# A block sum moved from GpSimd to an adding DMA, two splits moved ahead, and 64 bytes in front of a pair of tiles

## The chip, the cores and the metric

The kernel runs on one core of a Trainium2 chip. The time is that of one execution on the device, in microseconds; the median of three runs is given. The engines are TensorE (PE; PEld is its weight load), VectorE (DVE), ScalarE (ACT), GpSimd (POOL) and SyncE (SP). PE, DVE, ACT and POOL compute; SP issues transfers, and so does POOL, which here issues those that add to what is at their destination.

## What is computed

One layer of a decoder over 512 tokens and 16 learned tokens ahead of them, model width 1024, batch 1. Two branches read the same normalised input: retention (4 heads, keys of 256, values of 512) and gated linear attention (4 heads, keys of 128, values of 256). Their outputs are merged with sigmoid gates.

```python
u = rms_norm(h, norm_gain)
proj = u @ w_in
...
o_ret = retention_chunked(rq, rk, rv)
o_ret = head_group_norm(o_ret, ret_norm_gain.reshape(RET_HEADS, RET_V_DIM)).reshape(bsz, length, RET_WIDTH)
o_ret = o_ret * jax.nn.silu(rg)
...
o_gla = gla_chunked(gq, gk, gv, log_a)
o_gla = head_rms_norm(o_gla, gla_norm_gain.reshape(GLA_HEADS, GLA_V_DIM)).reshape(bsz, length, GLA_WIDTH)
o_gla = o_gla * jax.nn.silu(gg)

merged = jax.nn.sigmoid(m_ret) * (o_ret @ w_branch_ret) + jax.nn.sigmoid(m_gla) * (o_gla @ w_branch_gla)
return h + merged @ w_out
```

A final RMS norm follows. "The linear branch" below is `o_gla @ w_branch_gla`; "the heads' branch" is `o_ret @ w_branch_ret`.

## The kernel before

**Products in two parts.** Each float32 operand is split into a high part (a cast on ACT, L154) and a low part (the rest, a subtraction on DVE, also L154). A product is three matmuls: high by high, high by low, low by high. `split` makes both parts; `prepare` splits a weight block of 128x1024 and remembers the two instructions in `low`. The split weights rotate through three buffers for the high and three for the low parts.

**Seven products for eight.** `quad` multiplies two-by-two blocks by Strassen's scheme in Winograd's form: seven block products of 24 matmuls each, with sums of blocks on both sides. The weights' sums are made in place: w11 + x3, and w21 + w11 (L365), where x3 and x1 are themselves sums, made by a load from HBM by SP and a second load by POOL that adds (L280, L282). The other side's blocks and sums are the forms A11, A12, A22, S1, S2, S3, S4, here called `ga..` and `gs..`. The linear branch runs `quad` with `early=True` for two blocks of columns, j = 0 and j = 1, in the order of products 1, 7, 6, 2, 5, 4, 3. Three PSUM tiles, a, b and c (`bg_a`, `bg_b`, `bg_c`), collect them: product 6 adds to what product 1 left in b, after ACT has copied that out (L334), product 5 adds to b after the copy of product 6, product 4 adds to c after the copy of product 7. The copies go to two rotating buffers (`bg_x` in the trace, as the tiles x3 and x1 are). `put` adds a copy and a PSUM tile (L1160 to L1164) and sends the result to HBM.

**The forms of the linear branch.** `gla_sums` makes them while the branch already runs. `a00`, `a01`, `a10`, `a11` are the four blocks of the gated, transposed output of gated linear attention. The steps of `gla_sums` are woven with the products, one step after each product. `S2` is built from `a00`; after that `a01` becomes `a01 + a00` on POOL (L1115), and S4 is minus that sum: its high part on ACT (L1125), its low part on DVE (L1126). The forms S1 and A22 are placed behind the last weight split by `after`, which orders two instructions of one engine.

**The order of the work.** Instructions stand in each engine's queue in an order which the framework's planner works out from the program's order and its own cost estimates, unless `after` says otherwise. In the trace each engine runs its queue in that order, and an instruction that waits holds up those behind it.

**The heads' branch.** The turned (transposed) output of head h is kept in two tiles, `oh` and `ol`, of 8192 bytes a partition. Heads 0 to 2 share one pair in the pool `rp`, allocated at the first use in `ret_attention(0)`, the last tags of that pool; head 3's pair lies in the pool `cp`. `mm3` (L189, L192, L193) multiplies with them: the weights are stationary and `oh` or `ol` moves, 512 columns at a time, 8 products of 12 matmuls for each head.

## Time and profile before

| | |
|---|---|
| median of three runs | 761.6 us (761.6 to 762.16) |
| the profiled execution | 761.8 us, of which the span from the first to the last instruction is 760.0 us |
| PE busy | 749.8 us, 99% |
| DVE busy | 611.4 us, 80% |
| ACT busy | 450.8 us, 59% |
| POOL busy | 141.9 us, 19% |
| mean granted clock of PE | 0.997 |

In a timeline row stand the start and the length in us, the engine, the line, the operation, and what it writes and reads; in brackets the idle time before it and what ended that. A windows row gives, for a stretch of the span, the length, the busy time of each engine with the number of instructions that start there, the clock granted to PE, the busy share of the transfer engines and GB/s. In a row of waits stand the sum, the number and the longest. In a chain row stand start, length and what ran. In a row of transfers the last number is the time from issue to landing. A transfer's row on POOL shows the time in which POOL describes it, not the transfer itself. The ends of matmuls are modelled, so paces are read from starts.

### The profile page before, as it was taken

Reading aid. Unit: us, or ns where it says so; the run is one execution under the profiler, and the core shown is the slowest. Engines: PE = TensorE matmul, PEld = TensorE weight load, DVE = VectorE, ACT = ScalarE, POOL = GpSimd, SP = SyncE. Lnnn points to the kernel's source line nnn. Section 1 sums busy time; section 2 is a strip of 40 time slices with the busy share of each in tenths; the row PEclk is TensorE's granted clock in tenths of the full one; section 3 lists DMA queues with packets and bytes.
Section 4 is the critical chain, followed back from the end, with each engine's and each line's share of the span. In section 5 each row is a group of like instructions: output and inputs, shape, how many; then the busy total and the mean of one; then the engine's idle time right before and its main releaser. Section 6 shows DMA issues by size and latency. Waiting matters only on the chain.

```text
span 760.0 us, 14059 instructions
## 1 busy us (share of the span) xinstructions
PE 749.8 (99%) x5595; PEld 701.8 (92%) x5595; DVE 611.4 (80%) x873; ACT 450.8 (59%) x764; POOL 141.9 (19%) x172
## 2 busy tenths in 40 slices
PE   9999999999989999999999999999999999999996
PEld 6799899999989999999989999989999999988996
DVE  6799878689897789789957688966787989775994
ACT  7897584666974566546546555646464756532562
POOL 2211200112231122110530100440011210111142
PEclk9999999999999999999999999999999999999999
DMA  9864321822568972733783562794476356687503
GB/s 301 287 138 100 95 85 43 184 82 65 145 157 232 303 170 88 173 111 130 200 245 119 120 158 86 203 238 119 131 165 144 109 141 193 229 191 201 131 29 112
DMA packets 99994, 116.89 MB, mean 154 GB/s; under 512 B 5716, under 2 KB 90836, under 8 KB 99672
## 3 DMA queue, kind: packets, MB, share of 16 engines
q1 hardware_dynamic: 79896, 88.19, 36.7%
q0 software_dynamic: 19744, 27.27, 19.7%
q8 instruction: 44, 0.72, 0.4%
q10 hardware_dynamic: 288, 0.53, 0.2%
q14 instruction: 22, 0.18, 0.1%
HBM read 104.44 MB, written 11.53 MB: 153 GB/s over the span
## 4 chain that ended last, share of the span: by engine, by line
PE 91%; DVE 6%; issue 2%; ACT 1%; POOL 0%; POOLq 0%; DVEq 0%
PE rqk_b L318 6%; PE rv_b L318 6%; PE rg_b L318 6%; PE rqk_c L318 5%; PE br_p L189 4%; PE br_p L193 4%; PE br_p L192 4%; PE gg_b L318 3%; PE mr_b L318 3%; PE mg_b L318 3%; PE gv_p L640 3%; PE rv_c L318 3%; PE bg_b L318 3%; PE rg_c L318 3%; PE gg_c L318 2%
## 5 line engine op out<-in xcount | busy, mean ns | idle before, releaser
L189 PE MATMUL br_p<-oh,br_h 128*128 128x512 f32 x128 | 50.4, 394 | 0.0
L192 PE MATMUL br_p<-ol,br_h 128*128 128x512 f32 x128 | 50.4, 393 | 0.0
L193 PE MATMUL br_p<-oh,br_l 128*128 128x512 f32 x128 | 50.4, 393 | 0.0
L154 ACT CAST rv_h<-rv_w 128x1024 fp32r<-128x1024 f32 x24 | 25.3, 1052 | 27.1 <-DVE rv_w L371 9.6
L154 DVE TENSOR_TENSOR rv_l<-rv_w,rv_h 128x1024 fp32r<-128x1024 f32 x24 | 29.3, 1222 | 9.2 <-ACT rv_h L154 9.2
L154 DVE TENSOR_TENSOR rg_l<-rg_w,rg_h 128x1024 fp32r<-128x1024 f32 x20 | 24.4, 1222 | 8.7 <-ACT rg_h L154 8.7
L282 POOL DMA_DIRECT2D rqk_x<-in_w_in_dram x8 | 10.4, 1302 | 108.0 <-DVE rv_l L154 80.6
L154 ACT CAST rg_h<-rg_w 128x1024 fp32r<-128x1024 f32 x20 | 21.0, 1051 | 15.8 <-PE br_p L192 6.2
L193 PEld LDWEIGHTS br_p<-oh,br_l 128*128 128x128 f32 x128 | 24.0, 188 | 5.7
L189 PEld LDWEIGHTS br_p<-oh,br_h 128*128 128x128 f32 x128 | 24.0, 188 | 5.0
L192 PEld LDWEIGHTS br_p<-ol,br_h 128*128 128x128 f32 x128 | 24.0, 188 | 5.0
L154 ACT CAST br_h<-br_w 128x1024 fp32r<-128x1024 f32 x16 | 16.8, 1049 | 19.2 <-PE br_p L192 9.9
L154 ACT CAST rqk_h<-rqk_w 128x1024 fp32r<-128x1024 f32 x20 | 21.0, 1052 | 11.6 <-PE rqk_c L318 2.9
L1349 ACT ACTIVATE on<-av,nm,g_r 128x512 f32<-128x512 f32 x16 | 12.5, 780 | 25.4 <-DVE nm L1347 25.4
L318 PE MATMUL rv_b<-rv_l,fh 128*128 128x256 f32 x96 | 27.1, 282 | 0.2 <-DVE rv_l L154 0.2
L318 PE MATMUL rqk_b<-fh,rqk_h 128*128 128x256 f32 (+1 forms) x96 | 27.2, 283 | 0.0
L318 PE MATMUL rqk_b<-fh,rqk_l 128*128 128x256 f32 (+1 forms) x96 | 27.1, 283 | 0.0
L318 PE MATMUL rqk_b<-fl,rqk_h 128*128 128x256 f32 (+1 forms) x96 | 27.1, 282 | 0.0
L318 PE MATMUL rg_b<-rg_h,fl 128*128 128x256 f32 x96 | 27.0, 281 | 0.0
L154 DVE TENSOR_TENSOR rqk_l<-rqk_w,rqk_h 128x1024 fp32r<-128x1024 f32 x20 | 24.4, 1220 | 3.2 <-ACT rqk_h L154 3.2
L318 PE MATMUL rv_b<-rv_h,fl 128*128 128x256 f32 x96 | 27.0, 281 | 0.0
L318 PE MATMUL rg_b<-rg_h,fh 128*128 128x256 f32 x96 | 26.9, 281 | 0.0
(720 smaller groups left out, 3266.6 us busy)
## 6 DMA issues: line engine op xcount, KB each, us to landing
rv_w<-in_w_in_dram SPq DMA_DIRECT2D x16, 512.0 KB, 4.1
br_w<-in_w_branch_ret_dram SPq DMA_DIRECT2D x16, 512.0 KB, 3.4
rqk_w<-in_w_in_dram SPq DMA_DIRECT2D x12, 512.0 KB, 4.8
rg_w<-in_w_in_dram SPq DMA_DIRECT2D x12, 512.0 KB, 4.9
rqk_x<-in_w_in_dram SPq DMA_DIRECT2D x8, 512.0 KB, 3.9
rqk_x<-in_w_in_dram POOLq DMA_DIRECT2D x8, 512.0 KB, 8.2
rg_x<-in_w_in_dram SPq DMA_DIRECT2D x8, 512.0 KB, 3.7
rg_x<-in_w_in_dram POOLq DMA_DIRECT2D x8, 512.0 KB, 7.7
```

The source lines that it names most:

```text
L154: return nc.scalar.copy(hi, src), nc.vector.tensor_sub(lo, src, hi.bitcast(F32))
L189: m = nc.tensor.matmul(o, lh, rh, start=first, stop=False)
L192: nc.tensor.matmul(o, lh, rl, start=False, stop=False)
L193: m = nc.tensor.matmul(o, ll, rh, start=False, stop=last)
L282: x = nc.gpsimd.dma_start(t, block(0, 1), accum_op=ALU.add)
L318: m = nc.tensor.matmul(ps[t][:, :n] if wide else ps[t], l, r, start=first and j == 0, stop=kk == 3 and j == 2, skip_group_check=not fresh ...
L640: m = nc.tensor.matmul(pss[t], (al if j == 1 else ah)[t // 2, kh][:, k, c], (lo if j == 2 else hi)[:, kk, :], start=q == kk == j == 0, sto ...
L1349: nc.scalar.activation(on, ps, AF.Identity, scale=r, bias=nm)
```

## The change

The sum of two blocks is made by a transfer within SBUF that adds, issued by POOL: `a00 += a01` in place of `a01 += a00` on POOL's ALU. S4 is taken from `a00`, and its two instructions are placed behind the last weight split of their engines. In `quad` with `early=True`, the weights of product 5 are split right after those of product 2, ahead of w21 + w11, and the weights of product 3 right after those of product 4. At the first head, a tile of 64 bytes a partition is allocated ahead of `oh` and `ol` and set to zero by POOL.

```diff
@@ quad, early @@
             product(2, A12, w21, a, True)
-            nc.vector.tensor_add(w21, w21, w11)
+            ready = prepare(5, x1)
             put(0, 0, a, x)
             x7 = copy(c, 3)
             yield
+            nc.vector.tensor_add(w21, w21, w11)
...
-        product(5, S1, x1, b, False)
+        product(5, S1, x1, b, False, ready)
         put(1, 1, b, x7)
         run_late()
         yield
         product(4, A22, w21, c, False)
+        ready = prepare(3, w22) if early else None
         put(0, 1, c, y)
         yield
-        product(3, S4, w22, b, False)
+        product(3, S4, w22, b, False, ready)
@@ gla_sums @@
-        nc.gpsimd.tensor_add(a01, a01, a00)
+        nc.gpsimd.dma_start(a00, a01, accum_op=ALU.add)
...
         hi, lo = gforms[S4]
-        nc.scalar.mul(hi, a01, -1.0)
-        nc.vector.scalar_tensor_tensor(lo, a01, -1.0, hi.bitcast(F32), op0=ALU.mult, op1=ALU.subtract)
+        after(nc.scalar.mul(hi, a00, -1.0), low[0])
+        after(nc.vector.scalar_tensor_tensor(lo, a00, -1.0, hi.bitcast(F32), op0=ALU.mult, op1=ALU.subtract), low[1])
@@ ret_attention @@
+        if h == 0:
+            nc.gpsimd.memset(rp.tile([P, 16], F32, name="gap"), 0.0)
         oh, ol = [(rp if h < 3 else cp).tile([P, 4, T], F32R, tag=f"o{n}" if h < 3 else f"x{n}0", name=f"o{n}{h}")
                   for n in "hl"]
```

In the other branch of `quad` (without `early`) `ready` is set to `None` behind product 6, so nothing changes there.

## The prediction

> **What bounds the kernel now.** I read the page's busy shares and slices first, then the waits of PE, then the windows around the longest of them, then each engine's timeline there.

> ```profile
> PE 749.8 (99%) x5595; PEld 701.8 (92%) x5595; DVE 611.4 (80%) x873; ACT 450.8 (59%) x764; POOL 141.9 (19%) x172
> ...
> PE 91%; DVE 6%; issue 2%; ACT 1%; POOL 0%; POOLq 0%; DVEq 0%
> ...
> PE bg_b L318 <- DVE bg_l L154: 1.3, 1, 1.3
> ...
> PE bg_b L318 <- ACT bg_x L334: 0.8, 1, 0.8
> ```

> PE is busy for 99% of the span and holds 91% of the chain that ended last. A change can only gain by taking away one of PE's few waits or by making matmuls follow each other faster. Two of the three waits of 0.8 us or more stand next to each other, in the linear branch (tile `bg_b`); the third is at the start. The windows, cut where the granted clock changes, show that they cost more than their length:

> ```profile
> core 0: us, PE busy (x) PEld busy (x) DVE busy (x) ACT busy (x) POOL busy (x), PEclk, DMA share, GB/s
> 223.07:226.48 3.41, 1.43 (x10) 1.23 (x11) 3.41 (x5) 2.72 (x5) 0.00 (x0) 1.00 0.26 75
> 226.48:229.89 3.41, 3.41 (x19) 3.41 (x18) 3.09 (x4) 1.19 (x3) 0.00 (x0) 0.50 0.83 242
> 93.30:96.70 3.40, 2.93 (x21) 2.50 (x20) 3.27 (x10) 1.97 (x6) 0.99 (x2) 1.00 0.01 2
> ```

> PE was idle for 1.98 of the first 3.41 us, and through the next 3.41 us its clock was granted at 0.50 (19 matmuls started). An idle share of 0.47 us in 3.40 elsewhere left the clock at 1.00. Why PE waited is on the other engines:

> ```profile
> 218.67 1.22 DVE L154 TENSOR_TENSOR bg_l<-bg_w,bg_h 128x1024 fp32r<-128x1024 f32 x1
> 219.80 3.43 DVE L154 TENSOR_TENSOR gs<-og,gs 128x1024 fp32r<-128x1024 f32 x1
> 223.15 1.21 DVE L365 TENSOR_TENSOR bg_w<-bg_w,bg_w 128x1024 f32<-128x1024 f32 x1
> 224.29 1.21 DVE L154 TENSOR_TENSOR bg_l<-bg_x,bg_h 128x1024 fp32r<-128x1024 f32 x1
> ...
> 219.30 1.05 ACT L154 CAST bg_h<-bg_x 128x1024 fp32r<-128x1024 f32 x1
> 220.24 0.62 ACT L154 CAST ga22h<-og1gk 128x512 fp32r<-128x512 f32 x1
> 222.18 1.06 ACT L1125 ACTIVATE gs<-og1gq 128x1024 fp32r<-128x1024 f32 x1 [1.32 <-POOL og1gq L1115]
> 223.15 0.57 ACT L334 COPY bg_x<-bg_b 128x512 f32<-128x512 f32 x1
> ...
> 217.38 1.33 POOL L282 DMA_DIRECT2D bg_x<-in_w_branch_gla_dram  x1 [1.72 <-DVE gs L154]
> 218.84 3.30 POOL L1115 TENSOR_TENSOR og1gq<-og1gq,og 128x1024 f32<-128x1024 f32 x1
> ```

> The block sum on POOL (L1115) runs from 218.84 to 222.14. The DVE step that starts within it takes 3.43 us where the same form takes 1.22, and ends 1.1 us after POOL does: it stood still while POOL read SBUF. It pushes L365 and the low half of product 5's weights to 224.29, which is PE's wait of 1.3. ACT stands in front of L1125 for the same sum, and the copy of product 6's result, behind it in ACT's queue, is PE's wait of 0.8.

> **The change part by part.** *Block sum off POOL, product 5's weights split ahead.* The price of the jam is read from the same two products (2 and 5) of the next block of columns, which has no forms to make:

> ```profile
> 220.11 0.39 PE L318 MATMUL bg_a<-ga,bg_h 128*128 128x256 f32 x2
> ...
> 229.65 0.40 PE L318 MATMUL bg_c<-ga22h,bg_h 128*128 128x256 f32 x1
> ...
> 243.86 0.39 PE L318 MATMUL bg_a<-ga,bg_h 128*128 128x256 f32 x2
> ...
> 249.30 0.28 PE L318 MATMUL bg_c<-ga22h,bg_h 128*128 128x256 f32 x1
> ...
> 244.02 2.72 PE bg_a L318 x24
> ...
> 249.46 2.83 PE bg_c L318 x24
> ```

> 9.54 us against 5.44: 4.10 us too long, both waits and the half clock together (the last two rows, of the chain, give the length of one product of 24 matmuls). In the new order DVE runs, in steps of 1.13 (218.67 to 219.80): product 5's low half from 219.80, S1's low half from 220.95, done at 222.1. On ACT the casts of S1 and of x1 change places (x1's comes one step before 219.30), then come `ga22h` and, at about 220.9, the copy of product 6's result, with L1125 no longer ahead of it. PE wants product 5 at 222.83 (220.11 plus 2.72), so all 4.10 us go, if nothing else is late.

> *What is late next: product 4.* DVE has lost its slack. The steps that now come behind S1 and must be done before product 4:

> ```profile
> 225.42 0.68 DVE L154 TENSOR_TENSOR ga22l<-og1gk,ga22h 128x512 fp32r<-128x512 f32 x1
> 226.03 1.21 DVE L154 TENSOR_TENSOR bg_l<-bg_w,bg_h 128x1024 fp32r<-128x1024 f32 x1
> 227.16 0.68 DVE L1164 TENSOR_TENSOR gb<-bg_a,bg_x 128x512 f32<-128x512 f32 x1
> ...
> 227.87 0.59 ACT L334 COPY bg_x<-bg_c 128x512 f32<-128x512 f32 x1 [0.95 <-DVE gb L1164]
> ```

> L365 from 222.1, `ga22l` twice (0.60 each) to 224.45, L1164 to 225.1, product 4's low half to 226.25. The copy of product 7's result waits for L1164 (it needs the buffer that L1164 reads) and stands behind the cast of product 3's weights, which the change moves ahead (ACT to 225.4): done at 226.0. Product 5 ends at 225.55, so product 4 starts 0.5 us late, and its third matmul needs the low half at 226.25. If L1164 comes behind the low half, the copy ends at 226.8 and 1.25 us are lost; if it comes before `ga22l`, nothing. I take 0.6, between 0 and 1.3.

> *The sum as a DMA.* It needs S2's low half (the DVE step that released the row at 217.38) and stands in POOL's queue behind the accumulate at 217.38, so it is issued at 218.8, where the add starts now. No row shows an SBUF-to-SBUF add. The nearest are the accumulating loads of the same size, from issue to landing (issued at 206.7, 217.4 and 231.6):

> ```profile
> bg_x<-in_w_branch_gla_dram POOLq DMA_DIRECT2D x1, 512.0 KB, 5.8
> ...
> bg_x<-in_w_branch_gla_dram POOLq DMA_DIRECT2D x1, 512.0 KB, 6.5
> ...
> bg_x<-in_w_branch_gla_dram POOLq DMA_DIRECT2D x1, 512.0 KB, 10.4
> ```

> The middle one is just ahead of it in the same queue, with DMA share 0.26 after it; the slow one ran with the engines full. I take 7.5: landed at 226.3. S4's cast then runs behind the copy of product 7's result, from 226.3, and S4's low half on DVE behind product 3's low half (to 227.4) and L1162 (0.60, to 228.0): done at 229.2. Product 4 ends at 229.0 (225.55 + 0.6 + 2.83), so product 3 loses 0.2. A landing up to 226.95 costs no more; at 10.4 us (229.2) S4 is complete at 231.5, and 2.5 are lost instead of 0.2. No less than nothing is possible here.

> *Product 3's weights split ahead; L365 behind the split.* Both only change the order above: no instruction is added. In the next block of columns the split of x1 is bound by its landing:

> ```profile
> 242.12 1.05 ACT L154 CAST bg_h<-bg_x 128x1024 fp32r<-128x1024 f32 x1 [2.17 <-DMA bg_x<-in_w_branch_gla_dram]
> ...
> 225.53 0.37 SPq L280 DMA_DIRECT2D bg_x<-in_w_branch_gla_dram  x1
> ```

> It is ready at 244.45 and product 5 of that block starts at 246.58 (2.72 behind 243.86): 2.1 us of slack, where PE comes 3.3 earlier. But the load of x1 at 225.53 waits for L365 and the low half of product 5, which come 1.1 and 4.5 us sooner: some 1.5 us sooner on SP. I take 0, and 1.2 as the upper end (landing as now).

> *The 64-byte tile.* It is first used just ahead of `oh` and `ol` of heads 0 to 2, so it moves these two and nothing else that PE reads. Head 3's pair lies in another pool. Starts of PE's matmuls in the chain, head 2 and then head 3:

> ```profile
> 669.25 0.23 PE br_p L189
> ...
> 676.95 0.23 PE br_p L189
> 679.71 0.23 PE br_p L189
> ...
> 687.87 0.23 PE br_p L189
> ...
> 388.45 0.23 PE br_p L189
> ...
> 393.35 0.23 PE br_p L189
> ```

> Head 2: 11 groups of three matmuls in 7.70 us, 233 ns each. Head 3, same shape and same weights' buffers: 12 groups in 8.16 us, 227 ns. Head 0 (last two rows, 7 groups in 4.90): 233. So the pace hangs on where the moving operand lies. From the tiles' sizes `oh` and `ol` start at a multiple of 128 bytes, head 3's pair and the weights 64 bytes past one; 64 bytes bring heads 0 to 2 to head 3's place. 3 heads, 8 products of 12: 288 matmuls by 6.67 ns are 1.92 us, and PE is without a gap there. Bounds: 0, if the place is not the cause, and 1.92. [...]

> The tile's memset goes to POOL's queue:

> ```profile
> 249.88 0.87 POOL L1201 MEMSET km<- 128x256 f32 x1
> ```

> It has a sixteenth of that row's elements, so 0.87 is its upper end; POOL is idle 81% of the time. Cost 0; if it stood ahead of a head's power on POOL, 0.9 once.

> *Sum.* Gains 4.10 + 1.92, losses 0.6 + 0.2: 5.2 us. The profiled execution took 761.8 (span 760.0 and 1.8 around it), 0.2 above the median. 761.6 - 5.2 = **756.4**.

> **The rivals.** *The 64 bytes do nothing*: 758.3 (756.4 + 1.92). For it: head 3 also differs in its place in the program. Against: head 2 and head 3 stand within 20 us of each other at the two paces.

> *A new wait takes part of the place*: the sum lands late or L1164 and the copy come late, 2 to 2.3 us more (the 10.4 us row), and up to 4 with the half clock again (1.7 us: 3.41 at 0.50): 758.4 to 760.4. Whether it comes lies between the rows, 0.47 us idle without it and 1.98 with it. [...]

> *Slower: ACT queues S4's cast ahead of product 7's copy.* Then product 4 waits for the sum: it starts 1.74 us (1.06, 0.59 and a start) after the landing, at half clock after so long a wait (1.7). Against 229.65 before and with 1.92 gained, the point is a landing at 228.1, 9.3 us after issue; at 10.4 us the time is 762.7, and over 0.2% slower from 10.8 us. Against: the copy comes earlier in the program and its input (L1164) is ready first.

> *No change within 0.2%*: the PE lead made here is lost again to loads in the next blocks, whose transfers share engines that were 0.83 busy at 226.48: some 761. Against: the chain's rows at 244.02 and 249.46 stand 5.44 apart, twice 2.72, although x1 came off its load only at 242.12.

> **How the numbers follow.** Main case 0.60, with its own range 755.1 to 758.0 (losses from 0 to 2.4, product 6's small wait of 0.3 perhaps gone). The 64 bytes do nothing 0.10. New wait 0.19. Lead lost 0.06. Slower 0.05. About 0.2% (1.5 us) is what a measurement of this kernel can tell from no change. Of the new wait 0.03 lies above 760.1. Faster: 0.60 + 0.10 + 0.16 = 0.86; same 0.06 + 0.03 = 0.09; slower 0.05. The range 755.0 to 759.5 holds the main case, the first rival and most of the second.

> **What would show it.** Right: no PE wait over 0.3 us on product 5, no POOL add, every S1 low half at 1.2, L334 at 221, PEclk 1.00 through 226 to 230; heads 0 to 2 at 227 ns. Wrong: a PE wait on `bg_c` for L334 or on product 3 for S4, an ACT wait for the sum, a half-clock window about 226, heads 0 to 2 still at 233.

## The result, and the profile after

| | kernel before | kernel after |
|---|---|---|
| median | 761.74 us (761.6 to 762.16, 6 runs) | 758.16 us (757.25 to 759.11 but for one run, 6 runs) |
| ratio of times | | 0.9952, interval 0.9941 to 0.9963 |
| profiled execution | 761.8 us, span 760.0 | 759.11 us, span 757.3 |

One run of the kernel after took 4205 us, why is not known; it is left out of the ratio. In a second comparison the same kernel took 757.84 us (757.05 to 757.96, 5 runs), 0.9948 (0.9936 to 0.9961) of the kernel before. The change gains 3.6 to 3.8 us. The forecast was 756.4.

The profiled execution is the slowest of the runs counted, so it needs care. The busy shares and the shares of the chain, from its page:

```profile
PE 748.2 (99%) x5595; PEld 701.3 (93%) x5595; DVE 609.2 (80%) x873; ACT 450.4 (59%) x764; POOL 138.8 (18%) x173
...
PE 86%; DVE 6%; ACT 2%; DMA 2%; issue 2%; POOL 1%; POOLq 0%; DVEq 0%; ACTq 0%
```

PE still is the bound at 99%. POOL lost its add of 3.3 us. DMA has 2% of the chain, where before it had none: the chain now runs through the transfer that makes the sum. The waits of PE from 214 to 240 us (sum, times, longest):

```profile
PE bg_b L318 <- DVE gs L1129: 0.9, 1, 0.9
PE bg_c L318 <- ACT bg_x L334: 0.2, 1, 0.2
```

The waits of 1.3 and 0.8 us on product 5 are gone; a wait of 0.9 us on product 3, for S4's low half, is new. The same stretch by windows (the columns are those of the windows shown before; a number in brackets counts every instruction that runs in the stretch, also in part, and not only those that start there):

```profile
222.20:225.60 3.40, 3.40 (x32) 3.40 (x31) 3.40 (x5) 1.88 (x4) 0.00 (x0) 1.00 1.21 214
225.60:229.00 3.40, 3.19 (x26) 2.91 (x25) 3.40 (x5) 1.48 (x3) 0.00 (x0) 1.00 1.01 252
229.00:232.40 3.40, 2.52 (x21) 2.33 (x20) 2.50 (x4) 2.83 (x3) 0.00 (x0) 1.00 1.07 375
```

The clock stays at 1.00. PE is idle for 0.21 us ahead of product 4 and for 0.88 us in product 3. In the timeline (start, length, engine):

```profile
212.51 0.40 PE L318 MATMUL bg_b<-ga,bg_h 128*128 128x256 f32 x2
...
218.97 1.33 POOL L282 DMA_DIRECT2D bg_x<-in_w_branch_gla_dram  x1 [2.22 <-DVE gs L154]
219.78 1.44 POOL L1118 DMA_DIRECT2D og<-og1gq  x1
...
221.20 0.39 PE L318 MATMUL bg_a<-ga,bg_h 128*128 128x256 f32 x2
222.04 1.22 DVE L154 TENSOR_TENSOR gs<-og,gs 128x1024 fp32r<-128x1024 f32 x1
226.12 2.35 DVE L154 TENSOR_TENSOR bg_l<-bg_w,bg_h 128x1024 fp32r<-128x1024 f32 x2
226.40 0.57 ACT L334 COPY bg_x<-bg_c 128x512 f32<-128x512 f32 x1
227.02 0.39 PE L318 MATMUL bg_c<-ga22h,bg_h 128*128 128x256 f32 x1 [0.21 <-ACT bg_x L334]
228.89 1.06 ACT L1128 ACTIVATE gs<-og 128x1024 fp32r<-128x1024 f32 x1 [1.92 <-DMA og<-og1gq]
230.09 0.29 PE L318 MATMUL bg_b<-gs,bg_h 128*128 128x256 f32 x1
236.96 0.28 PE L318 MATMUL bg_c<-gs3h,bg_h 128*128 128x256 f32 x1
```

S1's low half is back at 1.22 us from 3.43. Products 2 and 5 take 5.82 us (221.20 to 227.02) instead of 9.54. The sum is issued at 219.78 and has landed when ACT goes on at 228.89; product 3 and the next block's product 1 take 6.87 us (230.09 to 236.96) instead of 5.71. From the block's product 1 to the next block's product 7 it is 24.45 us against 26.91: 2.46 gained.

The matmuls of the output branch of head 2, from the chain:

```profile
664.43 0.23 PE br_p L189
...
667.19 0.23 PE br_p L189
...
669.91 0.23 PE br_p L189
```

From 667.19 to 669.91 there are four groups of three in 2.72 us, 227 ns a matmul, where it was 233. The four groups before, the first of the product, still took 2.76, 230 ns. Over all 384 matmuls of the output branches the starts come to 89.00 us before and 87.43 after.

Where the gain of the profiled execution is: 2.46 in the linear branch, 1.31 from there to the end (the 1.57 of the output branches, less 0.03 to 0.04 in each of eight products that follow one, with a little back elsewhere), and 1.12 lost ahead of it, since product 1 starts at 212.51 instead of 211.39. Together 2.65, and the spans differ by 2.7. The 1.12 belong to the run and not to the change: in a second profile of the same kernel, shown below, product 1 starts at 211.69. The start of the program, by windows, before and then after:

```profile
5.30:6.90 1.60, 1.60 (x9) 1.29 (x8) 1.04 (x3) 0.85 (x2) 0.00 (x0) 1.00 1.03 367
```

```profile
5.30:6.90 1.60, 1.60 (x5) 1.21 (x5) 0.74 (x2) 0.68 (x2) 0.00 (x0) 1.00 0.96 333
```

Nine matmuls run in the one, in part or whole, and five in the other. The trace has the full clock granted from 4.6 us on before, and from 7.0 us on after (the column shows 1.00 also where no grant is recorded yet): in the run after, four matmuls took 2.02 us from start to start ahead of the grant (5.06 to 7.08) and 0.93 behind it (7.08 to 8.01). So 2.4 us more at about half the pace can cost some 1.2, an estimate from these rows, and 1.12 are lost.

### The profile page after: what moved, and what is told of

It is laid out like the page before. It is cut to its first block, busy times and chain, and to the rows that moved or that the text cites. A ratio compares the mean times of both kernels' runs of the same rounds, so it can differ in the third digit from the quotient of the medians.

```text
span 757.3 us, 14065 instructions
## 1 busy us (share of the span) xinstructions
PE 748.2 (99%) x5595; PEld 701.3 (93%) x5595; DVE 609.2 (80%) x873; ACT 450.4 (59%) x764; POOL 138.8 (18%) x173
## 4 chain that ended last, share of the span: by engine, by line
PE 86%; DVE 6%; ACT 2%; DMA 2%; issue 2%; POOL 1%; POOLq 0%; DVEq 0%; ACTq 0%
PE rqk_b L318 6%; PE rv_b L318 6%; PE rg_b L318 6%; PE rqk_c L318 5%; PE br_p L193 3%; PE br_p L189 3%; PE br_p L192 3%; PE gg_b L318 3%; PE gv_p L643 3%; PE mg_b L318 3%; PE rv_c L318 3%; PE rg_c L318 3%; PE mr_b L318 2%; PE bg_b L318 2%; PE gg_c L318 2%
## 5 line engine op out<-in xcount | busy, mean ns | idle before, releaser
L189 PE MATMUL br_p<-oh,br_h 128*128 128x512 f32 x128 | 50.0, 390 | 0.0
L154 ACT CAST rv_h<-rv_w 128x1024 fp32r<-128x1024 f32 x24 | 25.3, 1052 | 27.2 <-DVE rv_w L372 9.6
L154 DVE TENSOR_TENSOR rv_l<-rv_w,rv_h 128x1024 fp32r<-128x1024 f32 x24 | 29.3, 1221 | 9.2 <-ACT rv_h L154 9.2
L154 DVE TENSOR_TENSOR rg_l<-rg_w,rg_h 128x1024 fp32r<-128x1024 f32 x20 | 24.4, 1220 | 8.3 <-ACT rg_h L154 8.3
L154 ACT CAST rg_h<-rg_w 128x1024 fp32r<-128x1024 f32 x20 | 21.0, 1052 | 15.6 <-PE br_p L192 6.0
L282 POOL DMA_DIRECT2D rqk_x<-in_w_in_dram x8 | 10.4, 1302 | 105.4 <-DVE rv_l L154 80.6
L189 PEld LDWEIGHTS br_p<-oh,br_h 128*128 128x128 f32 x128 | 24.1, 188 | 4.5
L154 ACT CAST rqk_h<-rqk_w 128x1024 fp32r<-128x1024 f32 x20 | 21.1, 1053 | 11.5 <-PE rqk_c L318 2.9
L154 ACT CAST br_h<-br_w 128x1024 fp32r<-128x1024 f32 x16 | 16.8, 1050 | 18.7 <-PE br_p L192 9.5
L154 DVE TENSOR_TENSOR rqk_l<-rqk_w,rqk_h 128x1024 fp32r<-128x1024 f32 x20 | 24.4, 1221 | 3.9 <-ACT rqk_h L154 3.8
L318 PE MATMUL rv_b<-rv_l,fh 128*128 128x256 f32 x96 | 27.1, 282 | 0.2 <-DVE rv_l L154 0.2
L318 PE MATMUL rqk_b<-fh,rqk_h 128*128 128x256 f32 (+1 forms) x96 | 27.2, 283 | 0.0
L318 PE MATMUL rqk_b<-fh,rqk_l 128*128 128x256 f32 (+1 forms) x96 | 27.1, 282 | 0.0
L318 PE MATMUL rqk_b<-fl,rqk_h 128*128 128x256 f32 (+1 forms) x96 | 27.1, 282 | 0.0
L318 PE MATMUL rg_b<-rg_h,fl 128*128 128x256 f32 x96 | 27.0, 281 | 0.0
L318 PE MATMUL rv_b<-rv_h,fl 128*128 128x256 f32 x96 | 27.0, 281 | 0.0
L318 PE MATMUL rg_b<-rg_l,fh 128*128 128x256 f32 x96 | 26.9, 280 | 0.0
## 6 DMA issues: line engine op xcount, KB each, us to landing
rv_w<-in_w_in_dram SPq DMA_DIRECT2D x16, 512.0 KB, 4.2
br_w<-in_w_branch_ret_dram SPq DMA_DIRECT2D x16, 512.0 KB, 3.4
rqk_w<-in_w_in_dram SPq DMA_DIRECT2D x12, 512.0 KB, 4.8
rg_w<-in_w_in_dram SPq DMA_DIRECT2D x12, 512.0 KB, 4.5
rqk_x<-in_w_in_dram SPq DMA_DIRECT2D x8, 512.0 KB, 4.0
rqk_x<-in_w_in_dram POOLq DMA_DIRECT2D x8, 512.0 KB, 8.0
rg_x<-in_w_in_dram SPq DMA_DIRECT2D x8, 512.0 KB, 3.7
rg_x<-in_w_in_dram POOLq DMA_DIRECT2D x8, 512.0 KB, 7.8
```

The lines of the kernel that those rows point to most:

```text
L154: return nc.scalar.copy(hi, src), nc.vector.tensor_sub(lo, src, hi.bitcast(F32))
L189: m = nc.tensor.matmul(o, lh, rh, start=first, stop=False)
L282: x = nc.gpsimd.dma_start(t, block(0, 1), accum_op=ALU.add)
L318: m = nc.tensor.matmul(ps[t][:, :n] if wide else ps[t], l, r, start=first and j == 0, stop=kk == 3 and j == 2, skip_group_check=not fresh ...
```

## The experiments

All times are medians with their range; "ratio" is against the kernel before on the same chip, with its 95% interval. The table gives, for the profiled execution of each, the starts of products 2 to 4, of product 4 to 3 and of product 3 to the next block's product 7, the whole stretch from product 1 to there, and the time at which the full clock was first granted.

| kernel | median us | ratio | 2 and 5 | 4 | 3 and 1 | stretch | clock from |
|---|---|---|---|---|---|---|---|
| before | 761.7 | 1 | 9.54 | 2.94 | 5.71 | 26.91 | 4.6 |
| after | 758.16 | 0.9952 | 5.82 | 3.07 | 6.87 | 24.45 | 7.0 |
| after, again | 757.84 | 0.9948 | 5.81 | 3.07 | 5.75 | 23.34 | 5.2 |
| tile alone | 760.33 | 0.9983 | 9.67 | 2.83 | 5.57 | 26.78 | 4.0 |
| without tile | 759.37 | 0.9965 | 5.82 | 3.07 | 5.89 | 23.48 | 6.9 |
| tile of 32 bytes | 759.49 | 0.9971 | 5.72 | 3.07 | 5.86 | 23.44 | 4.4 |
| sum first | 757.20 | 0.9941 | 5.73 | 3.06 | 5.87 | 23.46 | 4.0 |
| sum first, again | 757.35 | 0.9941 | 5.73 | 3.06 | 5.76 | 23.33 | 5.2 |
| sum on POOL | 761.00 | 0.9994 | 8.60 | 3.07 | 5.87 | 26.32 | 7.2 |
| transfer alone | 765.48 | 1.0047 | 10.09 | 4.47 | 5.70 | 28.97 | 6.5 |
| transfer alone, pinned | 758.82 | 0.9959 | 6.12 | 2.93 | 5.68 | 23.51 | 4.9 |
| eviction late | 758.69 | 0.9966 | 6.86 | 2.94 | 5.69 | 24.19 | 6.7 |
| eviction late, pinned | 758.15 | 0.9954 | 6.85 | 2.94 | 5.57 | 24.06 | 7.0 |
| sum on DVE | 758.15 | 0.9953 | 6.06 | 3.70 | 5.76 | 24.29 | 5.9 |

**The tile alone** (kernel before, plus the tile):

```diff
+        if h == 0:
+            nc.gpsimd.memset(rp.tile([P, 16], F32, name="gap"), 0.0)
```

> The kernel before with the 64-byte tile alone; the linear branch is left as it was. Theory A (the pace of a 512-wide matmul hangs on where its moving operand and the next weights stand modulo 128 bytes): the output branches of heads 0 to 2 and head 3's pair go from 233 towards 227 ns, as in the trace after, where the products paid 1.56 us less: 759.8 to 760.2 us, against 761.7 before. Rival B (the address of an operand does nothing, and the pace after came with something in the linear branch): 761.7 us and 233 ns.

760.33 us (759.8 to 760.96), ratio 0.9983 (0.9974 to 0.9992): 1.34 us gained, a little less than theory A's 1.5 to 1.9. The output branches take 87.43 us, as in the kernel after. Rival B falls.

**Without the tile** (kernel after, those two lines taken out):

> The changed kernel without the 64-byte tile. Theory A: the linear branch keeps its 2.46 us (the stretch from its first product to the second block's product 7 took 24.45 us after, 26.91 before), the output branches go back to 233 ns: 759.2 to 759.6 us. Rival B (the tile does nothing): the same time as the changed kernel, 758.2. Rival C (the gain of the linear branch is partly one of the clock's phase in the profiled run): the trace shows the half clock elsewhere and the time lies above 760.

759.37 us (758.09 to 759.41), ratio 0.9965 (0.9951 to 0.9978), and the output branches are back at 89.00, as theory A has it; rivals B and C fall. The two parts add up: 1.34 and 2.30 make 3.64, and both together gain 3.6 to 3.8. The stretch gained 3.43 in this profile, 1 us more than in that of the kernel after: product 3 does not wait here.

**A tile of 32 bytes:**

```diff
-            nc.gpsimd.memset(rp.tile([P, 16], F32, name="gap"), 0.0)
+            nc.gpsimd.memset(rp.tile([P, 8], F32, name="gap"), 0.0)
```

> The changed kernel with a tile of 32 bytes in place of 64. Theory A in its narrow form (the two operands must stand at the same place modulo 128 bytes; now they stand at 32 and 64): 233 ns as before, 759.2 to 759.6 us, as without the tile. Rival D (any shift off the 128-byte line does it): 227 ns and 758.2 us.

759.49 us (758.76 to 760.17), ratio 0.9971 (0.9959 to 0.9982), the time without a tile. Head 2's branch in the chain:

```profile
664.17 0.23 PE br_p L189
...
666.97 0.23 PE br_p L189
```

Four groups in 2.80 us: 233 ns. Rival D falls, and theory A's narrow form fits. By the tiles' addresses in the built programs, with `oh` and `ol` at 0 or 32 bytes past a multiple of 128, and the weights at 64, a 512-wide matmul takes 233 ns; at 64 and 64 it takes 227. The shift by 32 bytes gained nothing (233 ns). That the two must stand at the same place is not shown, since no run moved the weights, and these runs do not show whether the weight load has a part in the two paces.

**The sum ahead of the load of x3** (kernel after; the load is the next block's, and stood ahead of the sum in POOL's queue):

```diff
+                    if t is x3 and name == "bg1":
+                        after(x, R["sum"])
...
-        nc.gpsimd.dma_start(a00, a01, accum_op=ALU.add)
+        R["sum"] = nc.gpsimd.dma_start(a00, a01, accum_op=ALU.add)
```

> The changed kernel with one order added: the adding load of x3 of the second block is issued behind the sum instead of ahead of it on the same queue. Theory A (product 3 lost 1.16 us because the sum, issued at 219.78 us and landed 9.1 us later, stood behind the 512 KB of that load): the sum is issued near 219.0, lands near 225.5, the pair of products that took 6.86 us goes back to 5.7 to 5.9, and the time is 757.0 to 757.3 us against 758.2. Rival B (product 3 waits for its evictions and VectorE's order, and not for the sum): 758.2. Rival C (the load of x3, now 1.4 to 6 us later, holds up the second block's product 7 at 237 us): 758.2 or more, with a wait of TensorE there.

757.20 us (756.86 to 757.9), ratio 0.9941 (0.9929 to 0.9954). Its timeline, and its transfers between 216 and 240 us (the last number is the time from issue to landing):

```profile
217.62 0.93 POOL L1120 DMA_DIRECT2D og<-og1gq  x1 [1.97 <-DVE gs L154]
218.24 1.66 POOL L282 DMA_DIRECT2D bg_x<-in_w_branch_gla_dram  x1
...
225.75 1.06 ACT L1130 ACTIVATE gs<-og 128x1024 fp32r<-128x1024 f32 x1
```

```profile
og<-og1gq POOLq DMA_DIRECT2D x1, 512.0 KB, 5.7
```

The sum lands after 5.7 us, against 8.9 in the kernel after, and ACT takes S4's part without a wait, right behind the copy of product 7. Product 3 and the next product 1 take 5.87 us, as theory A has it. Rival C falls too: the later load of x3 holds up nothing. But see the next run.

**The kernel after once more:**

> The changed kernel unaltered, beside the other three on one chip, to compare with. Its runs spread over 757.3 to 759.1 so far. If product 3's 0.9 us wait for the sum is one of the run (the sum landed 9.1 us after its issue in the profiled run of 759.1 us, and 8.8 us in the run without the tile, where no wait is seen), this profile shows a wait of 0 to 0.9 us there, and the span goes with that wait and with the moment at which the clock is granted at the start (4.0 to 7.0 us).

757.84 us (757.05 to 757.96). In the profiled execution (757.22 us) PE, from 205 to 240 us, waits for nothing but this:

```profile
PE bg_c L318 <- ACT bg_x L334: 0.2, 1, 0.2
```

```profile
227.03 1.06 ACT L1128 ACTIVATE gs<-og 128x1024 fp32r<-128x1024 f32 x1 [0.88 <-DMA og<-og1gq]
```

ACT still waits 0.88 us for the sum, but product 3 does not: S4's low half is ready just in time. So the 0.9 us wait was one of the first profiled run and not of every run; in the runs without the tile and with 32 bytes it was absent as well. The sum with x3's load ahead of it lands within about a microsecond of too late; the sum first lands with room.

**The best version.** The sum ahead of x3's load was run again, beside the last three below:

> The version with the sum ahead of the load of x3 once more, beside the others. If the sum's landing is what made the changed kernel's runs spread, this one again stays within 756.8 to 758.0 us, with no wait of TensorE ahead of product 3; if the 757.2 was luck of the chip, it comes out at 757.8 as the changed kernel did in its last comparison.

757.35 us (757.04 to 758.01), ratio 0.9941 (0.9929 to 0.9954), the same as the first time. It is the fastest of all versions, 0.5 to 1.0 us below the changed kernel. The intervals of the two overlap, so that it beats the changed kernel is likely and not shown; that it beats the kernel before is.

**The sum on POOL, the splits ahead kept:**

```diff
-        nc.gpsimd.dma_start(a00, a01, accum_op=ALU.add)
+        nc.gpsimd.tensor_add(a00, a00, a01)
```

> The changed kernel with the sum computed by GpSimd again (an add of the two tiles into a00), all else, the splits ahead too, as changed. Theory A (the jam came from the add on GpSimd, which held one VectorE instruction for 3.4 us): VectorE again shows one instruction of about 3.4 us near 219 us, product 5's parts come 2.2 us later than in the trace after, TensorE waits ahead of products 2 or 5, and 1.5 to 2.5 us of the 2.46 us of the linear branch are lost: 759.7 to 760.7 us. Rival B (the order of the splits was what made the jam): 758.2, and the 3.4 us are hidden by the lead.

761.0 us (760.6 to 761.75), ratio 0.9994 (0.9985 to 1.0003). Timeline and waits:

```profile
219.91 4.10 DVE L154 TENSOR_TENSOR bg_l<-bg_w,bg_h 128x1024 fp32r<-128x1024 f32 x1
219.99 2.93 POOL L1118 TENSOR_TENSOR og<-og,og1gq 128x1024 f32<-128x1024 f32 x1
```

```profile
PE bg_a L318 <- DVE bg_l L154: 2.2, 1, 2.2
```

The DVE step that began 0.08 us ahead of POOL's add took 4.10 us, 2.88 more than its usual 1.22, and the add took 2.93; the step ended 1.09 us behind the add: it stood still while POOL ran. This time it was the low half of product 2, and PE waited 2.2 us for it. All but 0.6 us of the linear branch's gain is gone (26.32 against 26.91), a little more than theory A had. This kernel has the tile and gained 0.65 us, against 1.34 for the tile alone, so the splits ahead by themselves gain nothing that these runs can show. By what the add holds up the DVE step, 2.88 us more beside an add of 2.93, is not shown.

**The transfer alone** (kernel before; the sum as a transfer, with S4's two instructions as in the change; no splits ahead, no tile):

```diff
-        nc.gpsimd.tensor_add(a01, a01, a00)
+        nc.gpsimd.dma_start(a00, a01, accum_op=ALU.add)
...
-        nc.scalar.mul(hi, a01, -1.0)
-        nc.vector.scalar_tensor_tensor(lo, a01, -1.0, hi.bitcast(F32), op0=ALU.mult, op1=ALU.subtract)
+        after(nc.scalar.mul(hi, a00, -1.0), low[0])
+        after(nc.vector.scalar_tensor_tensor(lo, a00, -1.0, hi.bitcast(F32), op0=ALU.mult, op1=ALU.subtract), low[1])
```

> The kernel before with the sum by the adding transfer (and S4's two parts ordered behind the last split, as changed), without the splits ahead and without the 64-byte tile. Theory A (the add on GpSimd was the cause): no instruction of 3.4 us on VectorE, products 2 and 5 take 6 to 7 us instead of 9.5, no half clock at 226 us: 759.4 to 760.2 us, near the 759.4 of the linear branch's change without the tile. Rival B (the splits ahead were needed): products 2 and 5 stay above 8 us, 761 or more.

765.48 us (763.28 to 766.02), ratio 1.0047 (1.0033 to 1.0061): slower than before. Rival B's two numbers came (above 8 us for products 2 and 5, above 761), but so did theory A's first sign, no DVE step of 3.4 us; the time went into a wait that neither had named. The timeline, PE's waits and three windows:

```profile
220.72 1.22 DVE L154 TENSOR_TENSOR gs<-og,gs 128x1024 fp32r<-128x1024 f32 x1
...
228.07 1.06 ACT L1125 ACTIVATE gs<-og 128x1024 fp32r<-128x1024 f32 x1 [3.85 <-DMA og<-og1gq]
229.03 0.60 ACT L154 CAST ga22h<-og1gk 128x512 fp32r<-128x512 f32 x1
229.54 1.04 ACT L154 CAST bg_h<-bg_w 128x1024 fp32r<-128x1024 f32 x1
230.49 0.58 ACT L334 COPY bg_x<-bg_c 128x512 f32<-128x512 f32 x1
```

```profile
PE bg_c L318 <- ACT bg_x L334: 4.0, 1, 4.0
```

```profile
224.96:228.38 3.42, 2.16 (x19) 1.95 (x17) 1.58 (x2) 0.31 (x1) 0.00 (x0) 1.00 0.98 256
228.38:231.79 3.41, 0.68 (x5) 0.68 (x6) 2.13 (x3) 3.41 (x5) 0.00 (x0) 1.00 1.02 337
231.79:235.20 3.41, 3.41 (x18) 3.41 (x17) 2.57 (x3) 0.23 (x1) 1.30 (x1) 0.50 0.56 127
```

ACT stood 3.85 us at S4's part, waiting for the sum, and behind it in the queue were a form's half, a weight split and the copy of product 7, for which product 4 waited 4.0 us; the half clock followed. This is the slower rival of the prediction, in a kernel without the splits ahead.

**The transfer alone, S4's part held behind that copy:**

```diff
+            R["x7"] = R["copy"]
...
+        after(m, R["x7"])
```

(`m` is S4's instruction on ACT and `R["x7"]` the copy of product 7's result.)

> The kernel before with the sum by the adding transfer alone, as in the run of 765.5 us, and S4's part on ScalarE held behind the copy of product 7. Theory A (that run lost its time to S4's part, which waited 3.85 us for the sum at the head of ScalarE's queue, ahead of the copy for which TensorE waited 4.0 us; the half clock followed): the wait and the half clock are gone, and the splits ahead are worth little by themselves: 759.3 to 760.3 us, against 759.4 with them. Rival B (the splits ahead are needed for more than this order): 761 or more.

758.82 us (758.48 to 758.87), ratio 0.9959 (0.9946 to 0.9973), with no splits ahead and no tile. From the timeline:

```profile
225.77 0.59 ACT L334 COPY bg_x<-bg_c 128x512 f32<-128x512 f32 x1 [0.90 <-DVE gb L1167]
227.07 1.06 ACT L1126 ACTIVATE gs<-og 128x1024 fp32r<-128x1024 f32 x1 [0.72 <-DMA og<-og1gq]
```

The one order is worth 6.7 us, and the stretch is 23.51 us, as with the splits ahead (23.48). So theory A holds, with a time 0.5 us under its range, rival B falls, and the splits ahead add nothing that shows. In the change they are what puts S4's part behind product 3's split on ACT, and behind the copy.

**Product 2's eviction later.** Two tries, both on the version with the sum first. The first put the eviction (DVE, 0.69 us) behind product 4's low half:

```diff
-            put(0, 0, a, x)
...
+        if early:
+            put(0, 0, a, x)
...
-                nc.vector.tensor_add(t, p, q)
+                x = nc.vector.tensor_add(t, p, q)
+                if th == 0:
+                    after(x, low[1])
```

> The changed kernel with the sum ahead of the load of x3, and VectorE's eviction of product 2 (0.69 us, in front of the low half of product 4) put behind that low half. Theory A (products 5 and 4 are late by 0.38 and 0.35 us, because of VectorE's order): product 4 waits for its low half 0.6 us less, the two products take 5.4 to 5.8 us instead of 5.97, and the time is 756.6 to 757.0 us, 0.2 to 0.6 under the 757.2 with the sum alone moved. Rival B (the 3.1 us are products slowed by something else than the low half): 757.2.

758.69 us (758.2 to 760.47), ratio 0.9966 (0.9954 to 0.9979). PE's waits:

```profile
PE bg_c L320 <- ACT bg_x L336: 1.3, 1, 1.3
PE rqk_c L320 <- ACT gb L1166: 1.1, 1, 1.1
```

PE waited 1.3 us for the copy of product 7, and 1.1 us in the next stage for an eviction on ACT. ACT had S4's part ahead of that copy. I took this order for the cause, pinned it, and kept the evictions' tiles and the second block as they were (the lines shown are those that differ from the first try, without the tiles'):

```diff
+        after(m, R["x7"])
...
-                if th == 0:
+                if th == 0 and j == 0:
                     after(x, low[1])
```

> As the run before it with VectorE's eviction of product 2 behind product 4's low half, now for the first block alone, with the tiles of the evictions as in the changed kernel, and with S4's part on ScalarE held behind the copy of product 7. In the earlier try the planner had put S4's part ahead of that copy, and TensorE waited 1.3 us for the copy, and 1.1 us more for an eviction that waited for a tile. Theory A (VectorE's order makes products 5 and 4 late): without those two waits products 5 and 4 take 5.5 to 5.7 us instead of 5.97, and the time is 756.7 to 757.1 us. Rival B (the rest of the lateness is elsewhere): 757.2 or more.

758.15 us (757.91 to 758.77), ratio 0.9954 (0.9941 to 0.9966). The timeline and PE's wait:

```profile
226.68 0.68 DVE L1175 TENSOR_TENSOR gb<-bg_a,bg_x 128x512 f32<-128x512 f32 x1
227.39 0.58 ACT L336 COPY bg_x<-bg_c 128x512 f32<-128x512 f32 x1 [0.94 <-DVE gb L1175]
```

```profile
PE bg_c L320 <- ACT bg_x L336: 1.2, 1, 1.2
```

My theory fell. The copy waits for the eviction itself, since it writes into the buffer that the eviction reads. The eviction late costs 1.1 us on product 4's start and saves 0.1 in product 4; the order kept is the better one. The prediction had this price: "If L1164 comes behind the low half, the copy ends at 226.8 and 1.25 us are lost".

**The sum on DVE** (kernel after; no transfer):

```diff
-        nc.gpsimd.dma_start(a00, a01, accum_op=ALU.add)
+        nc.vector.tensor_add(a00, a00, a01)
```

> The changed kernel with the sum computed on VectorE, in the place where it was on GpSimd. It costs VectorE one instruction of about 1.2 us (1.14 us of start to start) ahead of the low halves of products 2 and 5. Theory A (VectorE is the engine that sets products 2 to 4 of the first block): products 2, 5 and 4 together are 0.7 to 1.2 us later than in the changed kernel, product 3 waits for nothing: 758.5 to 759.2 us. Rival B (VectorE has that much time over): 757.2, the same as with the sum moved ahead.

758.15 us (757.94 to 758.9), ratio 0.9953 (0.9941 to 0.9966). The sum in the timeline, and PE's waits:

```profile
217.93 1.23 DVE L1118 TENSOR_TENSOR og<-og,og1gq 128x1024 f32<-128x1024 f32 x1
```

```profile
PE bg_c L318 <- DVE bg_l L154: 0.6, 1, 0.6
...
PE bg_a L318 <- DVE bg_l L154: 0.3, 1, 0.3
```

The 1.23 us of DVE come back as 0.9 us of PE's waits, on products 2 and 4, and the stretch is 24.29 us, 0.95 over that of the kernel after in its second run. DVE is the engine that sets these products, as theory A says; its time is a little under A's range. The transfer as changed gains no more than this (ratios 0.9952 and 0.9948), and ahead of x3's load a little more (0.9941): against POOL, either of the two other places tried does most of it.

## Why the prediction was nearly right, step by step

The ledger, against the second profile of the kernel after (757.22 us, where nothing disturbs product 3): 3.57 from the stretch, 1.31 from the tile, 0.30 lost at the start (product 1 at 211.69 instead of 211.39). 760.0 - 3.57 - 1.31 + 0.30 = 755.42, and the span is 755.4. Without the start the change gained 4.88 from trace to trace; the prediction's terms came to 5.2. The branch gave 0.27 more than forecast (3.57 against 4.10 less 0.6 and 0.2) and the tile 0.61 less, so that the two sums lie near each other is in part luck.

- *The jam, 4.10.* Right, and its cause is shown: with the add on POOL a DVE step takes 4.10 us again and the wait is back. That the splits ahead are part of the cure was argued in the prediction and is not so: without them the stretch is the same, if S4's part is kept behind the copy.
- *Product 4 late, 0.6.* Right: product 5 took 3.10 instead of 2.72, and product 4 3.07 instead of 2.83, together 0.62. Against the kernel before, though, where product 4 took 2.94, the loss is 0.51: the sum counted 0.11 of it twice. The trap named beside it (the eviction behind the low half, 1.25) cost 1.1 when it was tried.
- *The sum, 7.5 us to landing, product 3 late by 0.2.* The landing was too short: 8.4 to 8.9 us behind x3's load. Product 3 still lost only 0.04 to 0.18 in three profiles of four, and 1.16 in the first. There the whole branch ran 1.12 later, so the issue at 219.78 was not late; the sum landed 16.2 us after product 1's start, against 15.2 to 15.4 in the other three and 14.9 in the forecast. The price of a late landing was given, though for 10.4 us and a part of the rival.
- *The 64-byte tile, 1.92.* Mis-sized: 1.3. That the tiles' place sets the pace of these products is right (233 to 227 ns at the forecast place). But 6.67 ns for every one of 288 matmuls took for granted that each product runs at its settled pace from its first matmul. In half of the products of heads 0 and 1, and in the first of head 2, the 12 matmuls run at 230; that is 0.35 less. All of these stand behind a product of another kind, but so do four that run at 227, and why is open. The 0.03 to 0.04 us in each of eight products that follow a branch product, less what came back elsewhere, are 0.26 less again. The pace was read from head 3's rows from 679.71 on, past the first matmuls of its product.
- *From the profile to the median.* The sum of 5.2 was taken from the median before as if the profiled execution stood for every run. Over the 14 profiles of this case the full clock came between 4.0 and 7.2 us, 5.7 in the mean, and a microsecond costs up to a half (an estimate from the paces on both sides of the grant, 2.02 and 0.93 us for four matmuls). The profile before had it at 4.6, which is some 0.5 us better than the mean. That is about half of what lies between 756.9 (761.8 - 4.88) and the medians of 757.84 and 758.16. The rest stays open, and so does why the runs of the kernel before do not spread more with the start. Not all of them had the half clock of the profile: one window of it takes 0.0022 off a run's mean clock, and 13 of the 40 runs of the kernel before in the later comparisons show 0.999. They took 761.53 to 761.81 us and once 763.15, as long as the 14 at 0.997 or less (761.57 to 762.87). So the 4.10 of the jam was priced with a half clock that not every run pays, and what such a run pays in its place no trace of that kernel shows. A late start may be it: the kernel with the sum on POOL points there: its profiled run (761.11 us, clock from 7.2) had a wait of 2.2 us and no half clock, mean clock 0.999, and its ten other runs, at 0.996, took as long (760.6 to 761.75).
- *The slower rival, 0.05.* It did not come, but the run with the transfer alone shows how near it was: the same sum, with S4's part a few places earlier in ACT's queue, makes the kernel 3.8 us slower than before. The prediction set the deciding point at a landing 9.3 us after issue, at half clock; the wait came with 8.5, because there a form's half and a weight split stood between S4's part and the copy as well.
- *Two slips.* The low end of the main case, 755.1, should by its own terms be 755.3 (761.6 less 4.10, 1.92 and 0.3). And of the 19 matmuls in the half-clock window 16 start there; the others only run in it in part.

## What to carry to other kernels

The GpSimd add of this kernel cost what it stopped on VectorE (with the sum back on POOL, 2.88 us more on one step beside an add of 2.93), so look at the longest VectorE step beside such an instruction; here, taking it away was worth more than where its work went. When an operand comes from a transfer, place its first reader behind everything in that engine's queue that another engine waits for, and issue the transfer ahead of loads that have time; with its first reader ahead of such a copy the transfer alone lost 3.8 us, and ahead of x3's load it landed in 5.7 us instead of 8.9. And before the ends of a sum are put on one profiled execution, compare the clock at the start of that execution with other profiles (full clock from 4.0 to 7.2 us here).

## What the runs showed of the hardware

In the profile of the kernel before the granted clock changed 65, 66 and 221 times 3.413 us behind its first grant (4.62; 226.48, 229.89 and 758.96), in that of the kernel after 219 times (7.00; 754.52), and in that of the kernel with the tile alone 65 times (4.04; 225.91). Cut in steps of 3.413 us from the first grant, two windows of the kernel with the sum on POOL are

```profile
222.23:225.64 3.41, 1.58 (x13) 1.58 (x14) 3.41 (x3) 0.86 (x2) 0.69 (x1) 1.00 0.79 126
225.64:229.05 3.41, 3.41 (x32) 3.41 (x31) 3.41 (x5) 1.55 (x2) 0.00 (x0) 1.00 0.57 190
```

and two of the kernel with the tile alone:

```profile
222.49:225.91 3.42, 1.34 (x10) 0.94 (x9) 3.42 (x4) 2.73 (x5) 0.00 (x0) 1.00 0.22 27
225.91:229.32 3.41, 3.41 (x19) 3.41 (x18) 3.41 (x5) 1.56 (x3) 0.00 (x0) 0.50 0.86 275
```

The pace of the 512-wide matmuls of the output branches went here with the place of the moving operand modulo 128 bytes: 227 ns with it and the weights both at 64 (230 in nine products of the kernel after), 233 with it at 0 or at 32. Other matmuls did not go by it: in the linear branch of the kernel before, 256-wide ones with the moving operand at 0 and the weights at 64 run at 113 ns (product 2 of the second block of columns, 2.72 us for 24) or at 118 (product 4 there, 2.82 us), and those with both at 64 at 119 (product 1 of the first, 2.85 us). A transfer within SBUF that adds 512 KB took 5.7 to 5.9 us from issue to landing where it was issued ahead of the load of x3 (5.7 and 5.9 in the two profiles of the sum first, 5.9 in that of the eviction late), and 8.4 to 8.9 where it stood behind a load of 512 KB that adds (8.9 and 8.5 in the two of the kernel after, 8.6 without the tile, 8.4 with 32 bytes, 8.5 with the transfer alone).
